# Moving GpSimd's weight sums to VectorE in the second MLP product of a hybrid decoder, with half products and plain pieces in turn

## The chip, the cores and the metric

The kernel runs on one core of a Trainium2 chip. The metric is the time of one execution on the device in microseconds (us), the median of the runs shown. Engines are named as in the profile: PE is the matrix engine, PEld its weight loads, DVE the vector engine, ACT the scalar engine, POOL is GpSimd, SP is the queue that issues most DMAs. SBUF is the on-chip memory, PSUM the eight banks into which the PE writes.

## The reference: what is computed

A decoder trunk of two layers on 256 tokens and a model width of 2048, all float32. Layer 0 is a gated-linear-attention mixer, layer 1 a sliding-window attention mixer; after each comes an MLP:

```python
def sqrelu_mlp(h, w1, w2):
    u = jax.nn.relu(h @ w1)
    return (u * u) @ w2
...
h = h + sqrelu_mlp(rmsnorm(h, norm_mlp[layer]), mlp_w1[layer], mlp_w2[layer])
```

The hidden width of the MLP is 8192. The change is about `(u * u) @ w2`, a product of 256 x 8192 by 8192 x 2048 in each of the two layers.

## The kernel before: how the work is tiled and ordered

**Split weights.** Every weight block of 512 x 512 is loaded as a tile `ws` of [128, 4, 512] (four slices k of 128 rows) and split in two: `halve` (line 104) makes `wh`, a rounded copy by ACT (line 116), and `wl = ws - wh`, the residual, by DVE (line 117). Each of both instructions takes two slices, 128 x 1024 elements, so a block has two casts and two residuals. The PE then adds three products per slice: activation high part by `wh`, activation high part by `wl`, activation low part by `wh` (all recorded at line 80, the helper `mm`). `wh` and `wl` have four buffers of two slices each (`WHL = 4`), so splitting runs at most two blocks ahead of the PE. `ws` has three buffers (`WS = 3`). Loads and splits are traced under `high_priority(offset=WPRI)`, 60 steps ahead of their place in the program; the framework's scheduler then fixes the order on each engine.

**The MLP** (`mlp`, line 671). It runs over four groups g of 2048 hidden columns. For each group, four calls of `gemm_wide` make u; `evac_u` (line 833) reads the PSUM banks of the fourth (f = 0 to 3, in the tags tp, ms, tp, ms) with an ACT copy and a DVE addition each (lines 839 and 840), then multiplies, squares and splits them. Then `seven` (line 712) is called for n = 0 and n = 1, each for two column blocks c0, c1 of the output. I call the two calls together a stage; there are seven stages, four in the first MLP and three in the second (the last group of the second MLP goes by `gemm_wide` instead).

**`seven`.** The group's hidden rows are four row blocks. The first two by the two column blocks, with the two halves of the tokens, make a 2 x 2 by 2 x 2 block product, done with seven products instead of eight: `product(bank, o, weights)` is 12 matmuls of combination `o` of the activations with one weight tile. The row blocks 2 and 3 are done plainly: `plain(i, j, b0, b1)` is 24 matmuls, 12 for each half of the tokens, into two banks. With B11, B12, B21, B22 for the weight blocks, the products need B11, B22, B21, and the sums B11+B12, B22+B12, B11+B12+B22 and B11+B12+B22+B21. Two tiles hold the running sums: `x` (tag `wx`, two buffers) and `y` (tag `wy`, one). The order before (lines 785 to 819), each product written as bank and combination:

A0 with x = B11; E2 with y = B22; load B12 into a `ws` tile, x += B12 on DVE (line 795), y += B12 on POOL (line 796); B4 with x; x += B22 by an accumulating DMA from POOL's queue (`more`, line 730); plain(2,1) and plain(3,1) into E and F; C6 with y; D5 with x; x += B21 by an accumulating DMA; plain(2,0) and plain(3,0) into A and C; A1 with B21; C3 with x.

Between them DVE adds or subtracts the banks into the residual stream `xs` and the helper tile `v` (`add` and `sub`, lines 767 and 768). Banks A and C are of the PSUM tag `acc` (four buffers), E and F of `ms` (two), D of `tp` (two). In the last group (`final`), `done(c)` (line 770) squares the finished column blocks on ACT and books `operands` (line 614: transposes of `xs` and their scaled halves for the next layer) on later ticks; a product is one tick, a plain piece two. Before, they are booked for a pair of column blocks when both are done.

**Elsewhere.** `turn_x` (line 592) turns the input x into `xs`, tiles of pool `xp` (five buffers of four KB per partition); `last_x` (line 873) turns `xs` back for the output, also in `xp`.

Of the kernel before, what the change touches and what calls it, by code (L numbers as in the profile page):

```python
# [16 lines left out]
P = 128  # L17
# [31 lines left out]
def yoco_kernel(ctx: ExitStack, tc: tile.TileContext, x, norms, mlp_w1, mlp_w2, a_w_in, w_glr, w_gate, a_g_o, a_w_o,  # L49
# [3 lines left out]
    const = ctx.enter_context(tc.tile_pool(name="const", bufs=1))  # L53
    xp = ctx.enter_context(tc.tile_pool(name="xp", bufs=NC4 + 1))
    actp = ctx.enter_context(tc.tile_pool(name="actp", bufs=8))
# [47 lines left out]

    def halve(ws, o=C, n=2, between=None, low=None):

        halves = [(wp.tile([P, 2, C], F32R, name="wh", tag="wh", bufs=WHL),
                   wp.tile([P, 2, C], F32R, name="wl", tag="wl", bufs=WHL)) for _ in range(2)]
        with tc.high_priority(offset=WPRI):
            for k in range(0, 4, n):
                wh, wl = halves[k // 2]  # L110
                js, ks = slice(k % 2, k % 2 + n), slice(k, k + n)
                with ExitStack() as order:
                    if between:
                        for ins in between(k):
                            order.enter_context(tc.issue_after(ins.ins))
                    h = nc.scalar.copy(out=wh[:, js, :o], in_=ws[:, ks, :o])  # L116
                    l = (low or nc.vector).tensor_sub(out=wl[:, js, :o], in0=ws[:, ks, :o],  # L117
                                                      in1=wh.bitcast(F32)[:, js, :o])
                if between:
                    last[:] = h, l  # L120
        return halves

# [16 lines left out]
    def gemm_mov(src, act, evac, step=4):  # L139
# [3 lines left out]
        def run(kq):  # L143
# [4 lines left out]
            for k in range(4):  # L148
                wh, wl = (w[:, k % 2] for w in halves[k // 2])
# [14 lines left out]
    def gemm_sta(src, act, evac, widths=(P, P, P, P), step=4, first=(nc.sync,)):  # L164
# [4 lines left out]
        def run(kq):  # L169
# [4 lines left out]
            for k in range(4):  # L174
                wh, wl = (w[:, k % 2] for w in halves[k // 2])
                for f in range(nf):
# [16 lines left out]
    def gemm_wide(src, act, evac, last=False):  # L193
# [6 lines left out]
        def run(kq):  # L200
# [11 lines left out]
            for i, group in enumerate(groups):  # L212
                w = [[h[:, k % 2, f * P:(f + 1) * P] for h in halves[k // 2]] for k, f in group]
                for (k, f), (wh, _) in zip(group, w):
# [389 lines left out]

# [9 lines left out]
    def operands(acts, gains, c, b):  # L614
        tp = back(c, b)
        for a, g in zip(acts, gains):
            if b == 0:
                a.append(new_act())
            for j in range(2):
# [27 lines left out]
    def residual(w, act, gains, first=False):  # L647

        sq, r = new_norm()
        acts = [[] for _ in gains]  # L650
        runs = [gemm_mov(piece(w, c * C), act, add_to(c, acts, gains, sq, r)) for c in range(NC4)]
# [19 lines left out]
    def mlp(w1, w2, act, r, gains):  # L671
# [5 lines left out]
        sq, nr = new_norm() if gains else (None, None)  # L677
        acts = [[] for _ in gains]
        wide_tags.sort()
# [32 lines left out]
        def seven(w, n, op, us, g, final, acts, gains, sq, nr):  # L712
# [27 lines left out]
            def product(b, o, ws):  # L740
                p, st = use(b)
                halves = halve(ws)
                for k in range(4):
                    wh, wl = (h[:, k % 2] for h in halves[k // 2])
                    mm(p, op[o][:, 0, k], wh, st and k == 0, False, skip_group_check=True)
# [4 lines left out]

            def plain(i, j, b0, b1):

                halves = split_w([block(i, j)])
                ah, al, _ = us[i]
                ps_ = [use(b) for b in (b0, b1)]
                for k in range(4):
                    wh, wl = (h[:, k % 2] for h in halves[k // 2])
                    for t, (p, st) in enumerate(ps_):
                        tt = slice(t * P, (t + 1) * P)
                        mm(p, ah[:, k, tt], wh, st and k == 0, False, skip_group_check=True)  # L760
                        mm(p, ah[:, k, tt], wl, False, False, skip_group_check=True)
                        mm(p, al[:, k, tt], wh, False, k == 3, skip_group_check=True)
                    if k == 1:
                        tick()
                tick()

# [3 lines left out]
            def done(c):  # L770
# [14 lines left out]
            x = load(mp, "wx", 2, 0, 0)  # L785
            p = product("A", 0, x)
            if g == 0:
                nc.scalar.mul(out=v, in_=p, mul=-1.0)
            else:
                sub(v, p)  # L790
            y = load(mp, "wy", 1, 1, 1)
            product("E", 2, y)
            b12 = load(wp, "ws", WS, 0, 1)
            with tc.high_priority(offset=WPRI):
                nc.vector.tensor_add(out=x, in0=x, in1=b12)  # L795
                nc.gpsimd.tensor_add(out=y, in0=y, in1=b12)  # L796
# [25 lines left out]
        for g in range(4):  # L822
# [35 lines left out]
            for c in range(NC4):  # L858
# [247 lines left out]
```

## Time and profile before

| what | value |
|---|---|
| median of 3 runs | 2140.35 us (2140.31 to 2143.29) |
| the profiled execution | 2139.38 us, its span 2137.7 us |
| mean granted PE clock | 0.991 of full speed |
| busy share of the span | PE 97%, PEld 82%, DVE 68%, ACT 53%, POOL 11% |
| idle time of the PE | 67.8 us (span less 2069.9 us) |
| instructions | 27235 |

"Busy" is the time in which an engine has an instruction under way; the end of a matmul is modelled. In a row of the timeline the first number is the start in us from the start of the span, the second the duration, then engine, line, operation and tiles; in brackets stand the idle time before it and what ended it. In the groups, `x112` is a count, then come the busy time in us and the mean duration of one in ns. In a view by windows, after the length of the stretch come the busy time of each engine with its count, the granted PE clock, and the DMA share with GB/s.

### The profile page before, as it was taken

Reading aid. Unit: us, or ns where it says so; the run is one execution under the profiler, and the core shown is the slowest. Engines: PE = TensorE matmul, PEld = TensorE weight load, DVE = VectorE, ACT = ScalarE, POOL = GpSimd, SP = SyncE. Lnnn points to the kernel's source line nnn. Section 1 sums busy time; section 2 is a strip of 40 time slices with the busy share of each in tenths; the row PEclk is TensorE's granted clock in tenths of the full one; section 3 lists DMA queues with packets and bytes.
Section 4 is the critical chain, followed back from the end, with each engine's and each line's share of the span. In section 5 each row is a group of like instructions: output and inputs, shape, how many; then the busy total and the mean of one; then the engine's idle time right before and its main releaser. Section 6 shows DMA issues by size and latency. Waiting matters only on the chain.

```text
span 2137.7 us, 27235 instructions
## 1 busy us (share of the span) xinstructions
PE 2069.9 (97%) x10734; PEld 1747.0 (82%) x10734; DVE 1461.5 (68%) x1624; ACT 1142.3 (53%) x1560; POOL 243.9 (11%) x193
## 2 busy tenths in 40 slices
PE   9999999999999899999999999999899999999999
PEld 8988887887788688778877877788688778878888
DVE  6685444567757866876787677556866876786654
ACT  6645455555545545544556677545545544544543
POOL 1262111001100100110111133000200110110000
PEclk9999999999999999999999999999999999999999
DMA  7445555656774785676576443655685676576553
GB/s 272 146 144 182 180 178 184 212 181 190 212 241 158 216 257 194 188 229 212 152 213 174 157 138 118 237 181 173 197 267 186 181 242 211 157 209 206 191 190 128
DMA packets 210656, 410.57 MB, mean 192 GB/s; under 512 B 7024, under 2 KB 15232, under 8 KB 210528
## 3 DMA queue, kind: packets, MB, share of 16 engines
q1 hardware_dynamic: 194704, 377.51, 52.1%
q0 software_dynamic: 15104, 30.23, 8.3%
q8 instruction: 84, 1.38, 0.2%
q10 hardware_dynamic: 720, 1.09, 0.2%
q14 instruction: 44, 0.36, 0.0%
HBM read 406.71 MB, written 2.10 MB: 191 GB/s over the span
## 4 chain that ended last, share of the span: by engine, by line
PE 84%; DVE 10%; ACT 3%; issue 2%; DMA 1%; POOL 0%; ACTq 0%; SPq 0%; DVEq 0%; POOLq 0%
PE acc L80 53%; PE ms L80 18%; PE tp L80 11%; DVE wl L117 6%; ACT wh L116 1%; ACT sc L999 1%; DMA ws<-in_a_w_in_dram 1%; PE tp L610 1%; DVE wx L795 1%; DVE m L840 0%; PE tp L932 0%; DVE st L993 0%; DVE st L995 0%; DMA gk<-in_b_g_q_dram 0%; DVE xs L767 0%
## 5 line engine op out<-in xcount | busy, mean ns | idle before, releaser
L117 DVE TENSOR_TENSOR wl<-ws,wh 128x1024 fp32r<-128x1024 f32 (+1 forms) x636 | 780.5, 1234 | 479.5 <-ACT wh L116 474.9
L116 ACT CAST wh<-ws 128x1024 fp32r<-128x1024 f32 (+1 forms) x636 | 657.5, 1038 | 586.0 <-PE acc L80 440.2
L80 PE MATMUL acc<-wh,act 128*128 128x512 f32 x1792 | 574.8, 394 | 0.4 <-DVE xs L768 0.4
L80 PE MATMUL acc<-act,wh 128*128 128x512 f32 (+1 forms) x1664 | 412.6, 362 | 3.0 <-ACT wh L116 2.3
L80 PEld LDWEIGHTS acc<-wh,act 128*128 128x128 f32 x1792 | 336.3, 188 | 71.9 <-issue 2.0
L80 PE MATMUL acc<-wl,act 128*128 128x512 f32 x896 | 349.7, 390 | 0.0
L80 PEld LDWEIGHTS acc<-act,wh 128*128 128x128 f32 x1664 | 279.3, 190 | 30.5 <-ACT wh L116 2.5
L80 PE MATMUL acc<-act,wl 128*128 128x256 f32 x1408 | 256.4, 282 | 0.3 <-DVE wl L117 0.2
L80 PEld LDWEIGHTS acc<-act,wl 128*128 128x128 f32 x1408 | 226.3, 190 | 25.5 <-DVE wl L117 0.8
L117 DVE TENSOR_TENSOR wl<-wx,wh 128x1024 fp32r<-128x1024 f32 x112 | 189.9, 1705 | 81.5 <-ACT wh L116 80.3
L80 PE MATMUL tp<-act,wh 128*128 128x512 f32 x592 | 230.1, 394 | 0.0
L80 PE MATMUL ms<-act,wh 128*128 128x512 f32 x576 | 225.9, 394 | 0.0
L80 PEld LDWEIGHTS acc<-wl,act 128*128 128x128 f32 x896 | 168.7, 188 | 34.7 <-issue 1.7
L116 ACT CAST wh<-wx 128x1024 fp32r<-128x1024 f32 x112 | 117.5, 1055 | 130.4 <-PE ms L80 69.1
L796 POOL TENSOR_TENSOR wy<-wy,ws 128x2048 f32<-128x2048 f32 x14 | 64.1, 4579 | 883.9 <-DVE wl L117 883.9
L80 PE MATMUL ms<-wh,act 128*128 128x512 f32 x448 | 143.2, 393 | 6.5 <-DVE m L840 6.5
L80 PE MATMUL ms<-act,wl 128*128 128x256 f32 x576 | 148.6, 281 | 0.0
L80 PE MATMUL tp<-act,wl 128*128 128x256 f32 x576 | 148.3, 280 | 0.0
L80 PEld LDWEIGHTS tp<-act,wh 128*128 128x128 f32 x592 | 111.5, 189 | 13.3
L80 PEld LDWEIGHTS ms<-act,wh 128*128 128x128 f32 x576 | 108.6, 189 | 13.6
L80 PEld LDWEIGHTS tp<-act,wl 128*128 128x128 f32 x576 | 108.3, 189 | 12.7
L80 PEld LDWEIGHTS ms<-act,wl 128*128 128x128 f32 x576 | 108.5, 189 | 11.9
(230 smaller groups left out, 2282.2 us busy)
## 6 DMA issues: line engine op xcount, KB each, us to landing
ws<-in_mlp_w_dram SPq DMA_DIRECT2D x228, 1024.0 KB, 5.2
ws<-in_a_w_in_dram SPq DMA_DIRECT2D x44, 1024.0 KB, 5.0
wx<-in_mlp_w_dram POOLq DMA_DIRECT2D x28, 1024.0 KB, 9.4
ws<-in_a_w_o_dram SPq DMA_DIRECT2D x16, 1024.0 KB, 5.0
ws<-in_b_w_q_dram SPq DMA_DIRECT2D x16, 1024.0 KB, 5.0
ws<-in_b_w_o_dram SPq DMA_DIRECT2D x16, 1024.0 KB, 5.0
wx<-in_mlp_w_dram SPq DMA_DIRECT2D x14, 1024.0 KB, 5.1
wy<-in_mlp_w_dram SPq DMA_DIRECT2D x14, 1024.0 KB, 6.6
```

The lines of the kernel that those rows point to most:

```text
L80: nc.tensor.matmul(o, lhsT=l, rhs=r, start=start, stop=stop, **kw)
L116: h = nc.scalar.copy(out=wh[:, js, :o], in_=ws[:, ks, :o])
L117: l = (low or nc.vector).tensor_sub(out=wl[:, js, :o], in0=ws[:, ks, :o], in1=wh.bitcast(F32)[:, js, :o])
L610: nc.tensor.transpose(out=tp[:, j, t], in_=xs[c][:, t, (2 * b + j) * P:(2 * b + j + 1) * P], identity=ident)
L795: nc.vector.tensor_add(out=x, in0=x, in1=b12)
L796: nc.gpsimd.tensor_add(out=y, in0=y, in1=b12)
L999: nc.scalar.activation(out=sc[:, h], in_=sc[:, h], func=AF.Exp, bias=nmx[:, h:h + 1], scale=f[:, h:h + 1], accum_out=su[:, h:h + 1])
```

## The change

It does six things. In `halve`, `wl` becomes one tile of four slices with three buffers. In `seven`, the order becomes: A0 with x = B11; x += B12 by an accumulating DMA; plain(2,1); E2 with y = B22; load B12, y += B12 on DVE; plain(3,1); D4 with x; x += B22 by an accumulating DMA; C6 with y; plain(2,0), which does the 12 matmuls of bank A ahead of the 12 of bank C; plain(3,0); D5 with x into the same bank as D4; load B21, x += B21 on DVE; A1 with B21; C3 with x. Product 4 is now read once, into x21, instead of into x12 and x22, since bank D carries it on into v. `done` books the transposes of each column block by itself. `turn_x` does both halves' transposes before it takes the `xs` tile, and `xp` has four buffers; `last_x` takes its tile from the MLP's pool under the tag of `u`.

```diff
-    xp = ctx.enter_context(tc.tile_pool(name="xp", bufs=NC4 + 1))
+    xp = ctx.enter_context(tc.tile_pool(name="xp", bufs=NC4))
...
-    def halve(ws, o=C, n=2, between=None, low=None):
+    def halve(ws, o=C, n=2, between=None):
-        halves = [(wp.tile([P, 2, C], F32R, name="wh", tag="wh", bufs=WHL),
-                   wp.tile([P, 2, C], F32R, name="wl", tag="wl", bufs=WHL)) for _ in range(2)]
+        whs = [wp.tile([P, 2, C], F32R, name="wh", tag="wh", bufs=WHL) for _ in range(2)]
+        wl = wp.tile([P, 4, C], F32R, name="wl", tag="wl", bufs=WS)
...
-                    l = (low or nc.vector).tensor_sub(out=wl[:, js, :o], in0=ws[:, ks, :o],
-                                                      in1=wh.bitcast(F32)[:, js, :o])
+                    l = nc.vector.tensor_sub(out=wl[:, ks, :o], in0=ws[:, ks, :o], in1=wh.bitcast(F32)[:, js, :o])
...
-        return halves
+        return [(whs[k // 2][:, k % 2], wl[:, k]) for k in range(4)]
...
     def turn_x(c):
 
-        xs[c] = xp.tile([P, NT, C], F32, name="xs", tag="xt")
+        tps = [bank([P, 4, P], "tp") for _ in range(NT)]
         for t in range(NT):
-            tp = bank([P, 4, P], "tp")
...
             for k in range(4):
-                nc.tensor.transpose(out=tp[:, k, :], in_=src[:, k], identity=ident)
-            nc.scalar.copy(out=xs[c][:, t], in_=tp.rearrange("p k n -> p (k n)"))
+                nc.tensor.transpose(out=tps[t][:, k, :], in_=src[:, k], identity=ident)
+        xs[c] = xp.tile([P, NT, C], F32, name="xs", tag="xt")
+        for t in range(NT):
+            nc.scalar.copy(out=xs[c][:, t], in_=tps[t].rearrange("p k n -> p (k n)"))
...
-            def plain(i, j, b0, b1):
+            def plain(i, j, b0, b1, apart=False):
 
                 halves = split_w([block(i, j)])
                 ah, al, _ = us[i]
                 ps_ = [use(b) for b in (b0, b1)]
...
+                order = [(k, t) for k in range(4) for t in range(NT)]
+                for n, (k, t) in enumerate(sorted(order, key=lambda kt: kt[1]) if apart else order):
+                    wh, wl = halves[k]
+                    p, st = ps_[t]
...
+                    if n % 4 == 3:
                         tick()
...
                 turn.append(c)
-                if len(turn) % 2 == 0:
-                    for i, cc in enumerate(sorted(turn[-2:])):
-                        for b in range(2):
-                            later(1 + 2 * i + b, lambda b=b, cc=cc: operands(acts, gains, cc, b))
+                for b in range(2):
+                    later(2 + b, lambda b=b: operands(acts, gains, c, b))
...
             x = load(mp, "wx", 2, 0, 0)
             p = product("A", 0, x)
+            more(x, 0, 1)
             if g == 0:
                 nc.scalar.mul(out=v, in_=p, mul=-1.0)
             else:
                 sub(v, p)
+            plain(2, 1, "E", "F")
             y = load(mp, "wy", 1, 1, 1)
             product("E", 2, y)
             b12 = load(wp, "ws", WS, 0, 1)
             with tc.high_priority(offset=WPRI):
-                nc.vector.tensor_add(out=x, in0=x, in1=b12)
-                nc.gpsimd.tensor_add(out=y, in0=y, in1=b12)
-            p = product("B", 4, x)
-            more(x, 1, 1)
-            add(x12, p)
-            add(x22, p)
-            for i in (2, 3):
-                plain(i, 1, "E", "F")
+                nc.vector.tensor_add(out=y, in0=y, in1=b12)
+            plain(3, 1, "E", "F")
             add(x12, banks["E"])
             add(x22, banks["F"])
+            p = product("D", 4, x)
+            more(x, 1, 1)
+            add(x21, p)
             sub(x22, product("C", 6, y))
+            for i in (2, 3):
+                plain(i, 0, "A", "C", i == 2)
             add(v, product("D", 5, x))
-            more(x, 1, 0)
             if final:
                 add(x12, v)
                 add(x22, v)
                 done(c1)
                 sub(x21, v)
-            for i in (2, 3):
-                plain(i, 0, "A", "C")
-            product("A", 1, load(wp, "ws", WS, 1, 0))
+            b21 = load(wp, "ws", WS, 1, 0)
+            with tc.high_priority(offset=WPRI):
+                nc.vector.tensor_add(out=x, in0=x, in1=b21)
+            product("A", 1, b21)
             add(x11, banks["A"])
             add(x21, product("C", 3, x))
             if final:
                 done(c0)
...
-                        later(1 + i, lambda c=c + i // 2, b=i % 2: last_x(c, b))
+                        later(1 + i, lambda c=c + i // 2, b=i % 2: last_x(c, b, mp))
...
-    def last_x(c, b):
+    def last_x(c, b, mp):
 
         if b == 0:
-            xt[c] = xp.tile([P, 4, T], F32, name="xt", tag="xt")
+            xt[c] = mp.tile([P, 4, T], F32, name="xt", tag="u")
```

The other lines of the diff only take `wh` and `wl` of a slice from the new list that `halve` returns, and make the lists of `acts` dictionaries.

More of the change, by code (lines that the diff above doesn't have):

```diff
@@ L148, in run @@
             for k in range(4):
-                wh, wl = (w[:, k % 2] for w in halves[k // 2])
+                wh, wl = halves[k]
                 for t in reversed(range(NT)):
@@ L174, in run @@
             for k in range(4):
-                wh, wl = (w[:, k % 2] for w in halves[k // 2])
+                wh, wl = halves[k]
                 for f in range(nf):
@@ L212, in run @@
             for i, group in enumerate(groups):
-                w = [[h[:, k % 2, f * P:(f + 1) * P] for h in halves[k // 2]] for k, f in group]
+                w = [[h[:, f * P:(f + 1) * P] for h in halves[k]] for k, f in group]
                 for (k, f), (wh, _) in zip(group, w):
@@ L617, in operands @@
             if b == 0:
-                a.append(new_act())
+                a[c] = new_act()
             for j in range(2):
@@ L649, in residual @@
         sq, r = new_norm()
-        acts = [[] for _ in gains]
+        acts = [{} for _ in gains]
         runs = [gemm_mov(piece(w, c * C), act, add_to(c, acts, gains, sq, r)) for c in range(NC4)]
@@ L677, in mlp @@
         sq, nr = new_norm() if gains else (None, None)
-        acts = [[] for _ in gains]
+        acts = [{} for _ in gains]
         wide_tags.sort()
@@ L743, in product @@
                 for k in range(4):
-                    wh, wl = (h[:, k % 2] for h in halves[k // 2])
+                    wh, wl = halves[k]
                     mm(p, op[o][:, 0, k], wh, st and k == 0, False, skip_group_check=True)
@@ L755, in plain @@
                 ps_ = [use(b) for b in (b0, b1)]
[L756 to L763, printed above, removed]
+                order = [(k, t) for k in range(4) for t in range(NT)]
+                for n, (k, t) in enumerate(sorted(order, key=lambda kt: kt[1]) if apart else order):
+                    wh, wl = halves[k]
+                    p, st = ps_[t]
+                    tt = slice(t * P, (t + 1) * P)
+                    mm(p, ah[:, k, tt], wh, st and k == 0, False, skip_group_check=True)
+                    mm(p, ah[:, k, tt], wl, False, False, skip_group_check=True)
+                    mm(p, al[:, k, tt], wh, False, k == 3, skip_group_check=True)
+                    if n % 4 == 3:
                         tick()
-                tick()
             add = lambda o, p: nc.vector.tensor_add(out=o, in0=p, in1=o)
```

2 lines of the change are left out of this document (1 added, 1 removed).

## The prediction

> **What bounds the kernel now.** I read the page first, then the waits of the PE, then the timeline of the two halves of one stage, then windows over all seven stages.
>
> ```profile
> span 2137.7 us, 27235 instructions
> PE 2069.9 (97%) x10734; PEld 1747.0 (82%) x10734; DVE 1461.5 (68%) x1624; ACT 1142.3 (53%) x1560; POOL 243.9 (11%) x193
> ```
>
> The PE is the bound nearly everywhere: 67.8 us of its span are idle. Its waits say where:
>
> ```profile
> PE acc L80 <- DVE wl L117: 41.6, 15, 4.1
> PE ms L80 <- DVE m L840: 6.5, 7, 1.0
> PE tp L610 <- DVE act L243: 3.9, 1, 3.9
> PE acc L80 <- ACT wh L116: 3.7, 7, 2.3
> ```
>
> Most is one kind of wait: the PE stands ready for a residual `wl`. The view of the tile wx, under "who waited for it", puts 14 of the 15 on work on x, one in each call of `seven`:
>
> ```profile
>   PE acc L80: 41.4, 14
> ```
>
> The timeline of the third stage shows what makes them late, first for n = 0, then for n = 1 (the rows of different engines come from views by engine):
>
> ```profile
> 871.55 0.40 PE L80 MATMUL acc<-wh,ops 128*128 128x512 f32 x1
> 873.72 4.62 POOL L796 TENSOR_TENSOR wy<-wy,ws 128x2048 f32<-128x2048 f32 x1 [109.62 <-DVE wl L117]
> 874.17 0.41 DVE L840 TENSOR_TENSOR m<-tp,m 128x256 f32<-128x256 f32 x1
> 874.30 0.19 PEld L80 LDWEIGHTS ms<-wh,ops 128*128 128x128 f32 x1 [0.25 <-DVE m L840]
> 874.50 6.06 DVE L117 TENSOR_TENSOR wl<-wx,wh 128x1024 fp32r<-128x1024 f32 x2
> 879.48 0.50 PE L80 MATMUL acc<-wl,op 128*128 128x512 f32 x1 [1.89 <-DVE wl L117]
> 881.62 0.68 DVE L844 SCALAR_TENSOR_TENSOR m<-m,rb 128x512 f32<-128x512 f32 x1
> 883.36 0.41 DVE L840 TENSOR_TENSOR m<-ms,m 128x256 f32<-128x256 f32 x1
> 883.92 0.47 PE L80 MATMUL ms<-wh,act 128*128 128x512 f32 x1 [0.96 <-DVE m L840]
> ```
>
> ```profile
> 920.76 4.54 POOL L796 TENSOR_TENSOR wy<-wy,ws 128x2048 f32<-128x2048 f32 x1 [22.44 <-DVE wl L117]
> 921.14 6.38 DVE L117 TENSOR_TENSOR wl<-wx,wh 128x1024 fp32r<-128x1024 f32 x2
> 926.44 0.79 PE L80 MATMUL acc<-wl,op 128*128 128x512 f32 x1 [4.09 <-DVE wl L117]
> ```
>
> Each time two residuals take 6.1 to 6.4 us while POOL forms y += B12. Undisturbed, one takes 1.22 us:
>
> ```profile
> L117 DVE TENSOR_TENSOR wl<-wx,wh x112: 1210/1225/5256, 500.9 to 1946.8; 128x1024 fp32r<-128x1024 f32 x112
> L796 POOL TENSOR_TENSOR wy<-wy,ws x14: 4539/4578/4618, 510.7 to 1907.1; 128x2048 f32<-128x2048 f32 x14
> ```
>
> So the DVE stands still until POOL's sum ends: 873.72 + 4.62 = 878.34, and two residuals of 1.22 after that give 880.8; the record ends at 880.56. For n = 1 the same sum gives 927.7, the record 927.52. Without POOL the first residual of n = 1 would have ended at 922.4, just when the PE wanted it (926.44 - 4.09 = 922.35). The wait is POOL's, not a lack of DVE time.
>
> The wait costs more than its length:
>
> ```profile
> 882.11:925.70 43.59, 39.03 (x170) 1.00 0.75 223
> 925.70:932.53 6.83, 6.09 (x14) 0.50 0.88 216
> 932.53:964.53 32.00, 32.00 (x142) 1.00 0.90 264
> ```
>
> After the 4 us wait the granted clock is 0.50 for 6.83 us; after the 1.89 us wait it stays at 1.00. So the price is best taken from whole stages, from A0 of n = 0 to the end of C3 of n = 1, each 360 matmuls:
>
> ```profile
> 871.55:964.53 92.98, 85.79 (x362) 69.24 (x361) 74.50 (x69) 48.94 (x52) 14.32 (x6) 0.96 0.75 220
> ...
> sum 646.34, PE 596.63 PEld 481.50 DVE 531.54 ACT 354.04 POOL 103.18; mean PE 85.23 PEld 68.78 DVE 75.93 ACT 50.58 POOL 14.74
> ```
>
> An undisturbed product, from the chain of waits, gives the unit:
>
> ```profile
> 942.94 2.72 PE acc L80 x12
> ```
>
> 2.72/12 = 0.2267 us a matmul, 81.6 us a stage, 571.2 for seven. The stages take 646.3; 16 transposes in the fourth are worth about 1.5, as four push the next matmul back by 0.35:
>
> ```profile
> 1121.88 0.60 PE L610 MATMUL tp<-ident,xs 128*128 128x128 f32 x4
> 1122.23 0.71 PE L80 MATMUL ms<-wh,act 128*128 128x512 f32 x2
> ```
>
> That leaves **73.6 us** lost, 10.5 a stage. This is more than all the idle time of the page, since matmuls at half clock count as busy. [...]
>
> **The change, part by part.**
>
> *POOL out of the sums.* Gone are 14 sums of 4.58 us on POOL and with them the blocked residuals: 112 x (1705 - 1225) ns = 54 us of DVE time, from the mean in
>
> ```profile
> L117 DVE TENSOR_TENSOR wl<-wx,wh 128x1024 fp32r<-128x1024 f32 x112 | 189.9, 1705 | 81.5 <-ACT wh L116 80.3
> L795 DVE TENSOR_TENSOR wx<-wx,ws 128x2048 f32<-128x2048 f32 x14 | 32.1, 2290 | 0.2
> L767 DVE TENSOR_TENSOR xs<-acc,xs 128x512 f32<-128x512 f32 x56 | 38.1, 684 | 0.0
> L116 ACT CAST wh<-wx 128x1024 fp32r<-128x1024 f32 x112 | 117.5, 1055 | 130.4 <-PE ms L80 69.1 <-PE acc L80 49.6 <-DVE wx L795 11.6
> ```
>
> [...]
>
> *DVE's new work.* Per call of `seven`: y += B12 (2.29) comes, the x sum moves from B12 to B21 (2.29 as before), one PSUM read (0.68) goes. Per stage the DVE had 75.9 us; less 54/7 = 7.7, plus 4.6, less 1.4, makes 71.4, against 81.6 of matmuls. Its worst stretch is plain(3,0), D5, A1, C3, the next A0 and plain(2,1): PE 2 x 5.44 + 4 x 2.72 = 21.8 us; DVE 12 residuals (14.7), the sum (2.3), four reads (2.7) = 19.7. It fits, since before it five products followed one another and now at most four, with plain pieces around them. Cost taken 0; from 0 up to 1.5 us a call, if the x sum is queued behind A1's residuals and C3's cast and residual (1.05 + 1.22) come that late.
>
> *Sums by DMA.* There are two accumulating DMAs a call as before. Each has the same cover: A0's residuals to D4 and D4's to D5 span plain, product, plain or product, two plains, 60 matmuls = 13.6 us, as B4 to D5 did.
>
> ```profile
> L730 POOL DMA_DIRECT2D wx<-in_mlp_w_dram x28: 1274/1292/1376, 517.9 to 1932.0; - x28
> ...
> DMA to landing us min/median/max: 8.8/9.4/11.0
> ```
>
> A0's last residual ends about when A0 starts (two blocks ahead of need), so the sum lands some 11 to 12.5 us into a call; D4 starts at 2.72 + 5.44 + 2.72 + 5.44 = 16.3 and its first cast and residual need 2.3. Hidden by 1.5 us or more; behind the waiting cast in ACT's queue stand only casts for later blocks. Cost 0. The bytes are the same: one load of B12 more, one of B21 less.
>
> *Reordered banks.* Here a new wait appears. plain(2,1) now follows A0 and needs bank F after three matmuls on E: 871.55 + 2.72 + 0.25 + 0.68 = 875.2. F is one of the two `ms` banks that `evac_u` is still reading. If the DVE does that read right after the one at 874.17, no wait; if it first does E2's two residuals and the line 844 operation, 874.50 + 2.45 + 0.68 + 0.41 = 878.0, a wait of 2.8 us, too short for the half clock (1.89 us left it at 1.00). The present order shows that read late (883.36), which speaks for the late end; that the scheduler can let the PE go on with E's other matmuls speaks for the early one. I take 1.0 a stage. Bank C: C6's read must end before the second half of plain(2,0), 12 matmuls = 2.72 us later; a residual or two and the read take 1.9 to 3.1, a wait of 0 to 0.4; I take 0.1 a call. D4's read has 60 matmuls of cover.
>
> *Three `wl` buffers.* `wl` follows `wh`, which still has four halves and so sets the pace: 0. *`turn_x`, `last_x`, `xp`:* off the stages, with whole matrix products as cover: 0, within 1 us either way. *`operands` booked singly:* one wait stands behind the fourth stage,
>
> ```profile
> 1155.38 0.22 DVE L907 SCALAR_TENSOR_TENSOR gkq<-gk 128x64 f32<-128x64 f32 x1 [4.46 <-DMA gk<-in_b_g_q_dram]
> 1161.70 1.09 PE L610 MATMUL tp<-ident,xs 128*128 128x128 f32 x4 [3.92 <-DVE act L243]
> ```
>
> The DVE waits for a small DMA and the transposes wait for the DVE. The column blocks now come in another order, half of the work earlier, the other half nearer to its use; the DMA stays. From -5.6 us (wait and half clock, 3.9 + 1.7) to +4; I take 0.
>
> **Sum.** Of 73.6 us, each stage keeps 0.25 (E) + 1.0 (F) + 0.2 (C) + 0.3 (small change) = 1.75, 12.3 in all. Gain 61.3: 2139.4 - 61.3 = 2078.1 for the profiled execution; the median lies 1.0 above it, so **2079 us**.
>
> **Rivals.**
> *F decides (0.17).* The read stands behind both residuals: 2.8 instead of 1.0 in each stage, 12.6 us more: 2092.
> *DVE becomes the bound late in each call (0.12).* For: 19.7 of 21.8 us, and in the two last groups three more additions (2.05). Against: the blocks that lead in. 1.5 to 1.8 a call, 14 calls: 21 to 25 more, about 2102.
> *Slower: the accumulating DMA comes late (0.05).* x now passes through it twice in a call ahead of the DVE sum, and D4's casts stand at the head of ACT's queue. From a landing of about 13.5 us after the issue the PE waits; at 18 us it waits 4.2 and loses 1.7 more at half clock, 5.9 x 14 = 83 us: 2162. Against: 11.0 is the most of 28. [...]
> *No gain (0.04).* The residuals come late from the DVE's load alone, and other waits of the same size take the place of the 41 us: 2140. Against it stands the 922.35 above.
>
> **How the numbers follow.** Forecast 0.62, own range 2064 to 2088. 0.2% (4.3 us) is about what a measurement of this kernel can tell from no change. Faster: 0.62 + 0.17 + 0.12 = 0.91; same 0.04; slower 0.05. The range: low end, only E's waits stay (1.8) and the wait behind the fourth stage goes (5.6): 2140.4 - 73.6 + 1.8 - 5.6 = 2063; high end, the late-DVE case (2102) and 3 of the 4 us by which the wait behind the fourth stage may grow, 2105.
>
> **What would show it.** Right: no POOL row but DMA issues in the stages; residuals of wx at 1.2 us without a 5 us maximum; stages of 82 to 85 us at clock 1.00; PE waits for `wl` near 0 and a wait of E or F on line 840 of 0 to 2.8 us a stage. Wrong: stages over 87 us, waits of casts on the DMA of wx, or half-clock stretches inside them.

## The result, and the profile after

The changed kernel takes **2090.72 us** (median of four runs, 2089.95 to 2092.54) against 2141.4 us for the kernel before on the same chip (2140.31 to 2143.29): a ratio of 0.9764, 95% interval 0.9747 to 0.9781. It is faster by 2.4%, 11.7 us above the forecast of 2079: inside the whole range of 2063 to 2105, but 2.7 us outside the 2064 to 2088 that the prediction gave for its own mechanism. The profiled execution took 2090.28 us, with a span of 2088.6.

The page of the changed kernel, span and busy time by engine:

```profile
span 2088.6 us, 26959 instructions
PE 2056.3 (98%) x10734; PEld 1738.8 (83%) x10734; DVE 1428.7 (68%) x1624; ACT 1146.7 (55%) x1560; POOL 177.0 (8%) x179
```

The idle time of the PE fell from 67.8 to 32.3 us. That is 35.5 of the 49.1 us that the span lost; the other 13.6 are for the most part matmuls that no longer run at half clock, since PE busy time went from 2069.9 to 2056.3 with the same 10734 matmuls. The mean granted clock says the same: 0.009 of full speed was missing over 2137.7 us and 0.003 over 2088.6, which is 19.2 against 6.3 us.

Its waits of the PE:

```profile
PE ms L80 <- DVE wl L117: 9.0, 8, 1.2
PE tp L610 <- DVE rv L644: 4.5, 1, 4.5
PE tp L931 <- ACT po L1015: 3.6, 3, 1.2
```

The 41.6 us for `wl` ahead of the products (bank `acc`) are down to 0.8. In their place stand eight short ones of 1.1 us ahead of a plain piece (bank `ms`), one in each stage and a second in the fourth, and below them a wait that was not there before: three times 1.2 us at line 931, in the attention.

The group of residuals of x, and the windows over the third and fourth stage with the sum over all seven (busy time by engine, then granted clock, DMA share and GB/s):

```profile
L117 DVE TENSOR_TENSOR wl<-wx,wh 128x1024 fp32r<-128x1024 f32 x112 | 135.9, 1223 | 73.1 <-ACT wh L116 71.2
```

```profile
855.73:939.39 83.66, 82.41 (x363) 67.35 (x361) 71.70 (x70) 49.36 (x52) 3.85 (x3) 1.00 0.81 241
1029.20:1117.47 88.27, 85.58 (x379) 68.40 (x377) 78.35 (x88) 57.57 (x76) 3.87 (x3) 1.00 0.71 199
...
sum 590.22, PE 580.03 PEld 472.49 DVE 508.67 ACT 355.83 POOL 26.95; mean PE 82.86 PEld 67.50 DVE 72.67 ACT 50.83 POOL 3.85
```

The mean residual went from 1705 to 1223 ns, the seven stages from 646.34 to 590.22 us, all at clock 1.00. So 56.1 us came out of the stages. But the span lost only 49.1. The part between the fourth and the fifth stage (the next layer's K, V and Q products and the attention) gave 6.6 back; here it is in the windows of the changed kernel, and then of the kernel before:

```profile
1117.47:1471.18 353.71, 340.29 (x1749) 276.80 (x1748) 227.20 (x311) 208.45 (x400) 54.05 (x48) 0.99 0.50 165
```

```profile
1147.79:1494.87 347.08, 337.99 (x1750) 276.68 (x1749) 226.82 (x308) 206.62 (x396) 53.18 (x41) 1.00 0.51 167
```

What is left in a normal stage is 83.66 - 81.61 = 2.05 us. Here 81.61 is 360 matmuls at 0.2267 us. The timeline of the third stage shows most of the rest (rows of DVE, then of PE, from views by engine):

```profile
861.55 2.29 DVE L795 TENSOR_TENSOR wy<-wy,ws 128x2048 f32<-128x2048 f32 x1
863.75 0.69 DVE L848 TENSOR_TENSOR act<-u,act 128x512 fp32r<-128x512 f32 x1
864.35 2.36 DVE L117 TENSOR_TENSOR wl<-ws,wh 128x1024 fp32r<-128x1024 f32 x2
866.62 0.42 DVE L839 TENSOR_TENSOR m<-ms,m 128x256 f32<-128x256 f32 x1
865.62 0.50 PE L80 MATMUL ms<-wl,act 128*128 128x512 f32 x1 [1.12 <-DVE wl L117]
866.66 1.00 PE L80 MATMUL ms<-wh,act 128*128 128x512 f32 x2
```

The DVE forms y += B12 (2.29 us) first and the residuals of plain(3,1) behind it; the PE stands for 1.12 us. The last read of an `ms` bank by `evac_u` (line 839, bank F) stands behind both, so plain(2,1) gets F only at 867.04, and the two matmuls at 866.66 take some 0.4 us longer than elsewhere. The sum that blocked from POOL now delays from the DVE's own queue.

### The profile page after: what moved, and what is told of

Its sections match the earlier page's. It is cut to its first block, busy times and chain, and to the rows that moved or that the text cites. A ratio compares the mean times of both kernels' runs of the same rounds, so it can differ in the third digit from the quotient of the medians.

```text
span 2088.6 us, 26959 instructions
## 1 busy us (share of the span) xinstructions
PE 2056.3 (98%) x10734; PEld 1738.8 (83%) x10734; DVE 1428.7 (68%) x1624; ACT 1146.7 (55%) x1560; POOL 177.0 (8%) x179
## 4 chain that ended last, share of the span: by engine, by line
PE 88%; DVE 7%; ACT 3%; issue 1%; DMA 1%; POOL 0%; SPq 0%; ACTq 0%; POOLq 0%; DVEq 0%
PE acc L80 55%; PE ms L80 19%; PE tp L80 13%; DVE wl L117 3%; ACT sc L998 1%; ACT wh L116 1%; PE tp L610 1%; DVE wy L795 1%; DVE m L839 0%; PE tp L931 0%; DVE st L992 0%; DMA ws<-in_a_w_in_dram 0%; DVE st L994 0%; DMA gk<-in_b_g_q_dram 0%; PE tp L559 0%
## 5 line engine op out<-in xcount | busy, mean ns | idle before, releaser
L117 DVE TENSOR_TENSOR wl<-wx,wh 128x1024 fp32r<-128x1024 f32 x112 | 135.9, 1223 | 73.1 <-ACT wh L116 71.2
L730 POOL DMA_DIRECT2D wx<-in_mlp_w_dram x28 | 36.1, 1289 | 1128.4 <-DVE wl L117 1026.7
L80 PEld LDWEIGHTS tp<-act,wh 128*128 128x128 f32 x592 | 111.5, 189 | 13.3
L80 PEld LDWEIGHTS ms<-act,wh 128*128 128x128 f32 x576 | 108.6, 189 | 13.6
```

Source lines behind the costliest of these rows:

```text
L80: nc.tensor.matmul(o, lhsT=l, rhs=r, start=start, stop=stop, **kw)
L117: l = nc.vector.tensor_sub(out=wl[:, ks, :o], in0=ws[:, ks, :o], in1=wh.bitcast(F32)[:, js, :o])
L730: nc.gpsimd.dma_start(out=ws, in_=block(i, j).rearrange("(k p) n -> p k n", p=P), accum_op=ALU.add)
```

## The experiments

Two theories stood at the start. **A**, the prediction's: POOL's sum was the cause, and the DVE's new work costs nothing but small waits. **B**: the new order of products did as much, because it keeps the sum away from residuals that are due. Later runs ask where the sum must stand, and who took the 6.6 us. To compare stages, I give "lost": the sum of the seven stages less 572.7 us (571.2 of matmuls and 1.5 of transposes). The kernel before lost 73.6, the changed one 17.5. It is read from one profiled execution of each kernel, which lies up to 2.8 us from the median of its runs. The kernel before ran on each chip beside the experiments, at 2139.6 to 2141.0 us.

| run | time, us | ratio to before, 95% | lost, us |
|---|---|---|---|
| changed kernel | 2090.7 | 0.9764 (0.9747 to 0.9781) | 17.5 |
| old order, sum on DVE | 2112.0 | 0.9865 (0.9848 to 0.9881) | 46.9 |
| new order, sum on POOL | 2107.3 | 0.9847 (0.9833 to 0.9862) | 32.7 |
| new order, sum on DVE, late | 2081.0 | 0.9724 (0.9709 to 0.9738) | 9.4 |
| new order, sum on POOL, booked late | 2107.3 | 0.9848 (0.9834 to 0.9861) | 32.6 |
| old order, sum on DVE, late | 2088.2 | 0.9755 (0.9742 to 0.9769) | 22.2 |
| changed, `wl` in four halves | 2087.0 | 0.9753 (0.9739 to 0.9768) | 17.5 |
| before, buffers of the change alone | 2144.9 | 1.0022 (1.0013 to 1.0031) | 74.8 |
| changed, operands in pairs | 2087.0 | 0.9755 (0.9741 to 0.9768) | 17.6 |
| changed, gk early | 2084.8 | 0.9741 (0.9728 to 0.9754) | 17.5 |
| changed, C not apart | 2092.9 | 0.9769 (0.9756 to 0.9782) | 18.0 |
| three edits together | 2071.5 | 0.9673 (0.9660 to 0.9686) | 5.1 |
| old order, late sum, gk early | 2084.2 | 0.9738 (0.9725 to 0.9752) | 22.2 |

### Engine and order, one at a time

The kernel before with only the engine of the sum changed:

```diff
-                nc.gpsimd.tensor_add(out=y, in0=y, in1=b12)
+                nc.vector.tensor_add(out=y, in0=y, in1=b12)
```

> The kernel before with one edit: y += B12 on DVE instead of POOL; the order of the products stays. Theory A (the PE waits because POOL's sum blocks the residuals): no pair of residuals of x takes over 3 us, no half clock in the stages, and only the DVE's own queue is left: in the call for n = 1 the first residual of B4 moves from 922.4 to about 924.7 against a PE that wants it at 922.35, a wait near 2.3 us; with 0.4 us in n = 0 and the small rest some 4 us a stage instead of 10.5, total about 2096 (2088 to 2106). Rival B (five products in a row load the DVE too much, whoever forms the sum; the new order is the gain): stages of 89 us or more, total over 2120.

Measured: 2112.0. Between the two, so neither holds as it stood: of 73.6 us lost 26.7 came back, 46.9 stayed. The timeline of its third stage says why (DVE, then PE):

```profile
866.79 2.28 DVE L796 TENSOR_TENSOR wy<-wy,ws 128x2048 f32<-128x2048 f32 x1
868.99 2.35 DVE L117 TENSOR_TENSOR wl<-wx,wh 128x1024 fp32r<-128x1024 f32 x2
870.26 0.50 PE L80 MATMUL acc<-wl,op 128*128 128x512 f32 x1 [2.38 <-DVE wl L117]
```

The sum stands ahead of B4's residuals, exactly where POOL's sum had blocked them, and the PE waits 2.38 us for them where it had waited 1.89 before. For n = 1 the gain is there: the single wait of 4.09 us becomes three short ones that push the matmuls back by 0.41, 0.22 and 1.39 us. The order A0, E2, B4 leaves no plain piece in between.

The other half is the changed kernel with the sum back on POOL (the same edit, reversed).

> The changed kernel with one edit: y += B12 on POOL again; order, buffers and the rest as changed. Theory A in its strict form (POOL's sum costs the same wherever it stands): 6 to 9 us a stage come back, total over 2130. Rival B (the new place hides it, since plain(3,1) and D4 follow instead of the product that waits for the DVE): residuals of plain(3,1) of 4 to 5 us appear in the trace, but the PE waits at most 2 us a stage for them, total 2080 to 2105.

Measured: 2107.3, 32.7 us lost. Again neither theory holds as it stood. B is near: in n = 1 a residual of plain(3,1) takes 4.6 us (at 910.08 in the third stage) and the PE waits only 0.12 us for it, but n = 0 costs more and the time lies above its 2105. So the new order alone, with POOL still in the sums, recovers 40.9 of the 73.6, more than the engine alone. In n = 0 the blocked instruction is another one. The third stage, POOL, DVE, ACT and PE:

```profile
865.12 4.94 POOL L795 TENSOR_TENSOR wy<-wy,ws 128x2048 f32<-128x2048 f32 x1 [7.43 <-DMA wx<-in_mlp_w_dram]
866.43 4.18 DVE L843 SCALAR_TENSOR_TENSOR m<-m,rb 128x512 f32<-128x512 f32 x1
870.65 0.63 ACT L844 ACTIVATE u<-m 128x512 f32<-128x512 f32 x1 [3.74 <-DVE m L843]
871.18 1.03 ACT L116 CAST wh<-ws 128x1024 fp32r<-128x1024 f32 x1
872.26 0.51 PE L80 MATMUL ms<-wh,act 128*128 128x512 f32 x1 [1.35 <-ACT wh L116]
```

Read it as a chain. POOL's sum runs from 865.12 to 870.06. An elementwise DVE instruction that takes 0.69 us in the changed kernel takes 4.18 and ends just behind it. ACT's square waits for that instruction, the cast of plain(3,1) stands behind the square in ACT's queue, and the PE waits for the cast. Here no residual is blocked, and the PE still pays.

### Where the sum stands

The changed kernel with the sum traced behind plain(3,1), and an order edge to that piece's last residual, which `halve` keeps in the list `resid` (lines not shown):

```diff
-            with tc.high_priority(offset=WPRI):
-                nc.vector.tensor_add(out=y, in0=y, in1=b12)
             plain(3, 1, "E", "F")
+            with tc.high_priority(offset=WPRI), tc.issue_after(resid[-1].ins):
+                nc.vector.tensor_add(out=y, in0=y, in1=b12)
```

> The changed kernel with y += B12 issued on DVE behind the residuals of plain(3,1) instead of ahead of them. Theory A (the 1.1 us wait of plain(3,1) in each stage, 1.34 from start to start, is the DVE's sum standing ahead of its residual): the wait for wl is gone, stages at 82.3, total 9 us less, about 2081. Rival B (the wait is from the cast or from the late read of bank F and moves to another row): stages at 83.3 to 84, total 2088 to 2091.

Measured: 2081.0. The third stage of this run, DVE:

```profile
860.00 0.42 DVE L842 TENSOR_TENSOR m<-ms,m 128x256 f32<-128x256 f32 x1
864.73 0.68 DVE L851 TENSOR_TENSOR act<-u,act 128x512 fp32r<-128x512 f32 x1
865.33 1.22 DVE L119 TENSOR_TENSOR wl<-ws,wh 128x1024 fp32r<-128x1024 f32 x1
866.46 2.29 DVE L799 TENSOR_TENSOR wy<-wy,ws 128x2048 f32<-128x2048 f32 x1
```

The residual goes first, the sum follows at once, and the PE's wait is gone: the third, fifth and sixth stages take 81.78 us, 0.17 above the matmuls. So the place of the sum made the 1.12 us wait. By which way is not separated: with the sum out of the way the read of F, too, comes early (860.00 here, 866.62 in the changed kernel), and the PE does plain(2,1) in F before it wants the residuals of plain(3,1). The first, second and seventh stages keep 1.7, 0.8 and 1.0 us. There ACT's casts stand for the accumulating DMA of x (9 times in the run, 30.2 us in all, with landings of up to 13.3 us), and the PE then waits 1.19, 0.32 and 0.32 us for a residual.

The same with the sum on POOL:

> The changed kernel with the y sum behind the residuals of plain(3,1), as in the run that put it there on the DVE (2081.0 us), but on POOL. Theory A (POOL's sum takes 4.6 us and the DVE stands still for all of it, wherever it is): it starts about 866.5 of the third stage, ends at 871.1, and the residuals of x for D4, which started at 868.7 there, start at 871.1 and are wanted at 870.9, so the PE waits some 1.4 us in each call, 14 x 1.4 = 20 us: 2101, stages of 84.5 to 85.5 us. Theory B (the harm of POOL is only that it stands ahead of residuals that are due; in a place without such, the engine does not matter): 2081 to 2085, stages under 83 us. Theory C (the waits are long enough for the half clock): over 2107, no better than POOL in its old place.

Measured: 2107.3, the same as with POOL in its old place, and for a reason that none of the three theories had:

```profile
865.54 4.94 POOL L799 TENSOR_TENSOR wy<-wy,ws 128x2048 f32<-128x2048 f32 x1 [7.43 <-DVE wl L119]
```

The sum did not move. The order edge did not hold it back on POOL: it starts at 865.54 (865.12 without the edge), ahead of the residuals of plain(3,1), which start at 872.66 and 874.41. So this run repeats the one above and tells nothing of a late sum on POOL. That stays open.

Then the late place in the old order: the kernel before with the sum on DVE and behind B4's residuals.

```diff
                 nc.vector.tensor_add(out=x, in0=x, in1=b12)
-                nc.gpsimd.tensor_add(out=y, in0=y, in1=b12)
             p = product("B", 4, x)
+            with tc.high_priority(offset=WPRI), tc.issue_after(resid[-1].ins):
+                nc.vector.tensor_add(out=y, in0=y, in1=b12)
```

> The kernel before (2139.6 us), its order of products and its buffers kept, with two edits: the y sum on the DVE (2112.0 us alone) and behind the residuals of B4, whose product stands right behind A0 and E2. Theory A (what the old order still lost with POOL out of the sums is the place of the y sum ahead of B4's residuals, 2.66 us of wait for n = 0 and 1.39 + 0.41 for n = 1 in the third stage): most of these waits go, the half clock with them, the stages come to 83 to 85 us and the time to 2082 to 2090, as good as the changed kernel. Theory B (the order of products itself is needed: three products in a row with one sum ahead of the third load the DVE beyond the PE's pace anyway): the waits return at B4 or at C6 and D5, stages of 86 us or more, 2100 or more.

Measured: 2088.2. Theory A holds: with its old order, buffers and booking, the kernel is as fast as the changed one (the intervals of the ratios, 0.9742 to 0.9769 and 0.9747 to 0.9781, overlap). Its DVE in the third stage, and the sum of its windows:

```profile
860.40 2.38 DVE L119 TENSOR_TENSOR wl<-wx,wh 128x1024 fp32r<-128x1024 f32 x2
862.70 2.28 DVE L801 TENSOR_TENSOR wy<-wy,ws 128x2048 f32<-128x2048 f32 x1
```

```profile
sum 594.93, PE 583.85 PEld 471.27 DVE 506.84 ACT 355.69 POOL 38.94; mean PE 83.41 PEld 67.32 DVE 72.41 ACT 50.81 POOL 5.56
```

The three values of "lost" for the old order are 73.6 (POOL), 46.9 (DVE, early), 22.2 (DVE, late); for the new order 32.7, 17.5, 9.4. The new order is worth 40.9, 29.4 and 12.8 us: the better the sum stands, the less. Order and place remove the same waits.

### Who took the 6.6 us

The changed kernel with `wl` again as four buffers of two slices:

```diff
-        wl = wp.tile([P, 4, C], F32R, name="wl", tag="wl", bufs=WS)
+        wls = [wp.tile([P, 2, C], F32R, name="wl", tag="wl", bufs=WHL) for _ in range(2)]
```

> The changed kernel with wl again as four buffers of two slices. The changed kernel lost 6.6 us between the fourth and the fifth stage (K/V projections and attention), 3.5 of it in three waits of the query transposes for ACT copies. Theory A (with three whole buffers the scheduler puts a weight residual ahead of the row sums of the attention's norm, and ACT and PE wait behind it): that part gets 3 to 6 us shorter, stages unchanged at 83.7, total about 2086. Rival B (the loss is from the transposes booked singly, or from nothing but the shift of the order): no change, 2091 within 2 us. The stages stay at 83.7 for both; if they get longer, the buffers matter there after all.

Measured: 2087.0; the part between the fourth and fifth stage is 351.25 us, 2.5 shorter (theory A asked for 3 to 6), the stages are unchanged, and the three waits at line 931 are gone. And the reverse, the kernel before with only the buffers of the change (three `wl` of four slices, and `xp`, `turn_x` and `last_x` as changed to make room):

> The kernel before (2140 us) with the buffers of the change alone: wl as three buffers of four slices, and with it, to make room, xp with one buffer less and the last x in mp. The order of the products, the y sum on POOL and the booking of the operands stay as in the kernel before. Theory A (three wl buffers cost time in the attention whatever the order in the stages): the part between the fourth and the fifth stage, 347.1 us before, is longer by 2.5 to 4 us, the stages stay at 646 within 4 us, and the time is 2142 to 2145. Theory B (they cost only together with the new order, which leaves the DVE in another order there): 2140 within 1.5 us, with that part at 347 to 348.

Measured: 2144.9, slower than before by 0.22% (0.13 to 0.31). The part is 350.49 us, 3.4 longer, and in the waits of the PE stands

```profile
PE tp L934 <- ACT po L1018: 3.6, 3, 1.2
```

which is line 931 of the changed kernel, to the digit. Three `wl` buffers cost 2.5 to 3.4 us in the attention under either order. In the changed kernel the DVE there does a free residual (line 117, at 1207.67 us) ahead of the head norm's reduction (line 922, at 1208.80); with four halves the reduction comes first (at 1207.98). A residual that may run earlier stands ahead of work that the heads need. Of the 6.1 us by which this run's profiled span is longer (2143.8 us), another 1.5 lie ahead of the first stage and 1.2 in the stages; what makes those was not followed.

The booking of `operands`, in pairs as before:

```diff
-                for b in range(2):
-                    later(2 + b, lambda b=b: operands(acts, gains, c, b))
+                if len(turn) % 2 == 0:
+                    for i, cc in enumerate(sorted(turn[-2:])):
+                        for b in range(2):
+                            later(1 + 2 * i + b, lambda b=b, cc=cc: operands(acts, gains, cc, b))
```

> The changed kernel (2090.7 us) with one part undone: the operands of the next stages are booked for two column blocks at a time, as in the kernel before. The fourth stage of the changed kernel has 6.66 us over its matmuls where the other six have 2.05; 1.5 of the 4.6 more are transposes, and two waits of 1.32 and 0.43 us stand where the DVE forms operands (line 242) ahead of a residual. Theory A (booked singly, half of the operands' work now falls into the fourth stage beside residuals that are due): the two waits go and the transposes with them, but that work then falls behind the stage, so 2088 to 2090 with a fourth stage of 85.5 to 86.5 us, and the part between the fourth and the fifth stage stays within 1 us of 353.7. Theory B (the booking decides the 6.6 us that this part has become longer): the part falls back to 348 or less and the time is 2085 or less. Theory C (the operands in pairs come late for the K and V products): over 2093.

Measured: 2087.0. No theory was right on both counts. The fourth stage stays at 88.33 us, so the booking is not what makes it long; the part after it falls to 350.07, by 3.6. The intervals of the ratios overlap (0.9741 to 0.9768), so this verdict rests on the traces. The traces also say where in the part each cost lies. The start of the transposes of `khl` (1186.31 before, 1159.15 in the changed kernel), ahead of which the PE waits in each of these runs, cuts it in two. Ahead of it lie 38.5 us before, 41.7 in the changed kernel, 38.1 with the operands in pairs and 38.5 with the buffers alone; behind it 308.6, 312.0, 312.0 and 312.0, and 308.6 again with `wl` in four halves. So the booking costs 3.6 us in the first piece and the buffers 3.4 in the second, in both directions. The run with four halves gained only 2.5 because its first piece is 1.0 longer; the half clock behind the wait for gk lasts 6.8 us there instead of 3.4.

The small DMAs of gk, issued at the start of the program instead of behind the fourth stage:

> The changed kernel with the two small DMAs of gk issued at the start of the program, into a buffer that lives through it, and nothing else. In the changed kernel the DVE waits 5.07 us for that DMA behind the fourth stage, the transposes of line 610 behind it wait 4.48 us, and after them the clock is 0.50 for 3.4 us. Theory A (this DMA is what the transposes wait for, and the half clock follows from the wait): the wait goes and the 1.7 us of half clock with it, 2090.7 - 6.2 = 2084.5, part between the fourth and the fifth stage 347.5. Theory B (behind the DMA stands something else that is nearly as late, such as the rsqrt of line 644 or the squares before it): less than half of it goes, 2088 to 2090.

Measured: 2084.8, with that part at 348.64, 5.1 less (347.5 was expected; the half clock now falls behind the next wait). In the changed kernel, then in this one, the DVE's instruction that needs gk:

```profile
1129.87 0.23 DVE L906 SCALAR_TENSOR_TENSOR gkq<-gk 128x64 f32<-128x64 f32 x1 [5.07 <-DMA gk<-in_b_g_q_dram]
```

```profile
1124.67 0.21 DVE L906 SCALAR_TENSOR_TENSOR gkq<-gk 128x64 f32<-128x64 f32 x1
```

The DVE no longer stands, and the 4.5 us wait of the transposes behind it is no longer in the list of waits. Theory A holds.

Plain(2,0) between its banks in turn:

```diff
-                plain(i, 0, "A", "C", i == 2)
+                plain(i, 0, "A", "C")
```

> The changed kernel (2090.7 us) with plain(2,0) between its two banks in turn, as all other plain pieces, and not one bank after the other. Theory A (the second bank C still holds C6's product, whose read by the DVE ends 1.9 to 3.1 us after C6): the PE wants C 0.68 us after C6 and not 2.72, and waits 1.2 to 2.4 us in each call, 17 to 34 us in 14 calls: 2107 to 2124. Theory B (the scheduler lets the PE go on with the other bank, or the DVE reads C at once): 2089 to 2093, the same within 0.1%.

Measured: 2092.9 (2089.6 to 2093.0); stages of 83.70 to 83.76 us instead of 83.65. Theory A falls and B holds: that edit of the change is worth 0.1 us a stage.

### Together

The changed kernel with the late sum, `wl` in four halves and gk early, the three diffs above:

> The changed kernel (2090.7 us) with three edits that were each timed alone: the y sum behind the residuals of plain(3,1) (2081.0, 9.7 us less), wl as four buffers of two slices (2087.0, 3.7 less) and the two small DMAs of gk at the start (2084.8, 5.9 less). Theory A (three separate causes at three places, so the gains add): 2090.7 - 19.3 = 2071.4, within 2070 to 2074, with stages near 82 us and the part between the fourth and the fifth stage at 345 to 346.5. Theory B (they share a cause, the order of the DVE's work at the end of the fourth stage and in the attention): 2076 or more.

Measured: **2071.5 us**, ratio 0.9673 (0.9660 to 0.9686): faster than both kernels, by 1% than the changed one. The gains add as theory A had it, though the part behind the fourth stage, 343.88 us, is shorter than its 345 to 346.5. Its windows:

```profile
852.60:934.37 81.77, 81.77 (x363) 67.52 (x361) 71.15 (x70) 49.14 (x52) 3.81 (x3) 1.00 0.83 246
1024.17:1111.13 86.96, 84.60 (x379) 68.68 (x377) 77.93 (x88) 57.34 (x76) 3.83 (x3) 1.00 0.71 203
...
sum 577.82, PE 575.46 PEld 473.68 DVE 504.81 ACT 354.08 POOL 26.77; mean PE 82.21 PEld 67.67 DVE 72.12 ACT 50.58 POOL 3.83
```

The PE is busy for all of the third stage; 5.1 us are left, 3.8 of them in the fourth stage, where the next layer's operands are made beside the products. And the old order with the late sum and gk early:

> The kernel before with its order of products, the y sum on the DVE behind B4's residuals (2088.2 us with these two edits) and now the two small DMAs of gk at the start as well. Against it stands the run with the new order and three edits together (2071.5 us), so the two differ in the order of the products and in what hangs on it. Theory A (the order still has a worth of its own once the sum is well placed: 84.6 us a stage against 81.8): the transposes' wait of 4.28 us and the half clock behind it go, 2088.2 - 5.9 = 2082.3, within 2080.5 to 2084.5, 9 to 13 us above the new order; the stages stay at 84.5 to 84.7. Theory B (the order has no worth beyond the place of the sum): 2074 or less.

Measured: 2084.2, stages of 84.5 to 84.7 as before. With the sum well placed, the order of the products and what hangs on it (the booking too) are worth some 13 us of the 70 between 2141 and 2071. In the two traces the stages differ by 17.1 us, and 2.0 go back behind the fourth stage.

## Why the prediction was right or wrong

**Right in sign and whole range, 11.7 us too fast, and outside the range of the forecast's own mechanism.** For the profiled execution the sum said 2078.1, the trace 2090.28. Of these 12.2 us, 5.2 lie in the stages (17.5 lost instead of 12.3), 6.6 in the part behind the fourth stage, 0.2 ahead of the first.

*POOL out of the sums.* The mechanism was right: residuals of x at 1223 ns, the 41.6 us of waits gone, no half clock in the stages. What failed is "the wait is POOL's, not a lack of DVE time", as the account of all 73.6 us. With the engine alone changed, 46.9 of them stayed, since 2.3 us of sum ahead of the residuals is late as well; 24.7 of these went when the sum stood behind them. The cause is a sum, on either engine, ahead of work that is due.

*DVE's new work, "Cost taken 0", up to 1.5 a call.* This is the step of the sum that failed in the stages. The sum costs 1.12 us of wait a stage (1.3 from start to start), in plain(3,1) of n = 0, not at A1 and C3 where the prediction had looked. The late-sum run takes it away. The stretch that I took for the worst, 19.7 of 21.8 us, cost nothing. A normal stage keeps 2.05 us where 1.75 were foreseen, and that these are so close is luck: 1.3 of them are a wait that the sum had at 0.

*F, 1.0 a stage.* Mis-sized: the read of F ends at 867.04, and the wait behind it is some 0.4 us. The read comes even later than in the prediction's late case, 11.3 us into the stage instead of 6.5, since the sum and the residuals of plain(3,1) stand ahead of it. The scheduler let the PE do E's other matmuls first; that brought plain(3,1) forward to where its residual was not ready. So the late read may have a part in the 1.12 us, which no run separates from the sum's. The rival "F decides" gave 2092, next to the measured time. Its late read occurred, its wait of 2.8 us did not, so its number is near by luck.

*C, 0.2 a stage.* Nothing of that size appears; the edit that was to keep it small is itself worth 0.1.

*Fourth stage.* It keeps 6.66 us where 1.5 for transposes and 1.75 were foreseen; 3.4 of the 5.2 us lie here. Beside the wait of every stage there are two more, of 1.16 us behind the sum and an operand of the next layer and of 0.27 us behind operands; the booking does not decide them. What makes the rest was not followed.

*Three `wl` buffers, cost 0, since `wh` "still has four halves and so sets the pace".* Wrong: 2.5 to 3.4 us, shown in both directions. I looked at the stages, where the pace is set by `wh`, and not at the attention, where a freer residual changes the DVE's order.

*`operands` booked singly, 0 from -5.6 to +4.* It cost about 3.6, near the end of the bounds. The wait for gk that the step named is real: 5.9 us when taken away.

*Accumulating DMAs, 0.* Right: no wait of the PE names them, and none took over 10.9 us to land (11.0 before). But two of the signs of being wrong that the prediction listed did show: ACT's casts wait for the DMA of wx five times, 5.4 us in all, where before they never did, and the fourth stage takes over 87 us. With the late sum the casts wait 30.2 us and the PE up to 1.19, so the rival of the late DMA is real, if small. POOL's issues took 1274 to 1376 ns, the same as before. The DVE that is overrun late in each call did not appear.

*"2.8 us, too short for the half clock".* This rested on one row, a wait of 1.89 us with the clock at 1.00 behind it, and does not hold: waits of 2.4 us were followed by the half clock in three stages of seven (see the last section).

## What to carry to other kernels

An engine whose mean load leaves room can still be late at one place: look at what stands in its queue directly ahead of an instruction that another engine is about to want, and move long work with a late use behind it, before you move it to another engine or reorder the program. Two edits that remove the same wait do not add, so try each alone before you credit one. A buffer that lets work start earlier can change the order on the engine that does it in other parts of the program too (here it cost 2.5 to 3.4 us in the attention), so compare the stages you did not touch as well.

## What the runs showed of the hardware

**In these runs the length of a wait alone did not tell whether the half clock followed.** The kernel before with its sum on the DVE has the same wait in front of B4 in each of its seven stages, 2.4 us. Two of them, and the 3.4 us behind each:

```profile
514.87 0.80 PE L80 MATMUL acc<-wl,op 128*128 128x512 f32 x1 [2.39 <-DVE wl L117]
693.45 0.50 PE L80 MATMUL acc<-wl,op 128*128 128x512 f32 x1 [2.40 <-DVE wl L117]
```

```profile
514.61:518.02 3.41, 3.15 (x8) 2.48 (x9) 2.60 (x5) 0.61 (x1) 1.36 (x1) 0.50 0.89 295
693.20:696.60 3.40, 3.15 (x14) 2.58 (x15) 3.20 (x6) 1.58 (x2) 1.27 (x1) 1.00 0.94 295
```

Eight matmuls against fourteen in the same time. In three of the seven stages the granted clock falls to 0.50 behind this wait, for 3.4, 6.8 and 3.4 us; in four it stays at 1.00. In the run with the new order and the sum on POOL, two waits shortly after one another (1.35 and 0.76 us in the third stage) leave the third stage at 1.00; the same two are followed by 3.4 us at half clock in the second and the sixth. So the same 2.4 us cost the clock in three stages and not in the other four. What decides between them was not shown.

**The GpSimd sum held up DVE work on other tiles than its own.** Beside y += B12 on POOL, in the third stage, it was a pair of residuals of x in the kernel before, 6.06 us at 874.50 and 6.38 at 921.14 against 1.22 for one undisturbed, and a multiplication of `m` in the run with the new order and the sum on POOL, 4.18 us at 866.43 instead of 0.69. Through ACT's queue that became a wait of the PE for a cast which had nothing to do with either. In the same stage two DVE additions that read a PSUM bank ran beside the sum (at 865.50 and 865.84) and took 0.42 and 0.68 us, as without it.
